# A chunked gated recurrence inside a projection kernel: its attention levels regrouped into tiles of 32 keys, with a compact block for the masked copies

## The chip, the cores and the metric

One NeuronCore of a Trainium2 chip. The metric is the device time of one execution in microseconds (us). Engines: TensorE (PE; its weight loads are PEld), VectorE (DVE), ScalarE (ACT), GpSimd (POOL), and SyncE (SP), which issues DMAs.

## The reference

One layer of a hybrid trunk over 2048 positions of 1024 channels, in float32: RMSNorm, one input projection, a pooling branch and a gated recurrence (HGRN2), each projected back and gated, an output projection, then a convolutional GLU feed-forward and a final norm. The change touches the recurrence alone. Its core, for each of 4 heads of 128 channels:

```python
f = lb + (1 - lb) * sigmoid(zf); k = 1 - f; q = silu(zq); v = zi
# S_t = diag(f_t) S_{t-1} + k_t v_t^T ;  o_t = S_t^T q_t , in chunks:
b = cumsum(log f)                               # inside a chunk
attn[t, s] = sum_k q[t,k] * exp(b[t,k] - b[s,k]) * k[s,k]   for s <= t
o = attn @ v + (q * exp(b)) @ state
state = exp(b_last) * state + (k * exp(b_last - b))^T @ v
```

## The kernel before, in words

The large projections are float32 products made of three fp32r matmuls each (high and low parts), in Strassen-like units of seven products; all of them are issued by one helper (L150), and the weights are split on the way by a ScalarE cast (L246) and a VectorE subtraction (L247). The sequence is worked in two halves of 1024 positions; each half has a mixer and a feed-forward part, and each mixer holds two blocks of 512 positions (four pieces of 128).

The recurrence runs as small tasks beside the mixer's projections: one `hgrn_task` for each of 4 heads and 4 blocks, 16 in all, up to three at a time, the two blocks of one head usually in step. Python generators stand for the tasks: after every six matmuls of the helper the loop advances each task that is due, and `yield n` means "not before n such ticks". So a task's instructions land between projection matmuls in the program, and `in_turn` holds a task's first matmul of a level behind the projection matmul that was issued last. A scheduler that simulates times sets the final order on each engine; each engine then works its queue in order.

Inside a task, q, k (`ks`) and the decays d (the f above) lie as channels by 512 positions. The 128x128 causal block `att` (keys by queries, four pieces side by side) is built by levels: at level h, queries of the upper half of each block of 2h positions meet keys of its lower half, with q and k scaled by the decays between. After each level q, k and d are updated, so that the next level needs only a product. Before the change the levels are:

- Levels 1 and 2 (L1106): four matmuls each, 128 keys by 128 moving columns; half of the columns also deliver the diagonal. Two masked copies from PSUM into `att`, each of 256 elements on 128 partitions (L1113, L1126).
- Levels 4+8 (`two_levels`, hh = 4): operands from ScalarE (L1042), GpSimd (L1043) and VectorE (L1044, L1047, L1049), in halves of two pieces. 16 matmuls (L1060) of 32 keys by 48 moving columns, in four groups of 32 PSUM partitions. 12 masked copies of 32 partitions by 64 elements (L1074). Then VectorE updates q, k and d.
- Levels 16+32 (hh = 16): the same with 8 matmuls of 64 keys by 96 columns and 6 masked copies of 64 partitions by 128 elements.
- Level 64: four matmuls of 64 keys by 64 columns (L1119) and one ScalarE copy (L1124), without a mask, as the whole rectangle is wanted.

Then k is transposed (L1140), the state products (L1149) and the outputs (L1165, L1167) follow, and the result goes to DRAM for the next projection. The masks are made at the start on GpSimd (`setup_task`, L638 to L656), between DMAs that accumulate weights (L167).

Of the kernel before, what the change touches and what calls it, by code (L numbers as in the profile page):

```python
# [13 lines left out]
U8 = mybir.dt.uint8  # L14
AF = mybir.ActivationFunctionType
ALU = mybir.AluOpType
AX = mybir.AxisListType

P = 128
# [11 lines left out]
NT = TB // P  # L31
# [41 lines left out]
AHEAD = 3  # L73
ADD_LAG = 3
# [9 lines left out]
def tile_trunk(  # L84
# [541 lines left out]
    def setup_task():  # L626
# [6 lines left out]
        keys = [(h, h, 0, h) for h in (1, 2, 4, 16)]  # L633
        keys += [(8 * h + t, 2 * h, t * h, h) for h in (4, 16) for t in range(2)]
        for key, x, off, w in keys:
            nb = 64 // x
            mf = mask_of()
            behind(pool.memset(mf, 1.0), last_root[0] if len(masks) < 6 else added[3])  # L638
            v = mf.rearrange("p (b h) -> p b h", h=x)
            pool.affine_select(out=v, in_=v, pattern=[[-2 * x, nb], [0, x]],  # L640
                               compare_op=ALU.is_ge, fill=0.0, base=-off, channel_multiplier=1)
            pool.affine_select(out=v, in_=v, pattern=[[2 * x, nb], [0, x]],
                               compare_op=ALU.is_ge, fill=0.0, base=off + w - 1,
                               channel_multiplier=-1)
            m8 = const.tile([P, 64], U8, tag=f"m{key}", name=f"m{key}")
            yield 2
            pool.tensor_copy(m8, mf)
            masks[key] = m8.rearrange("p (b h) -> p b h", h=x)
        for t in range(2):
            mf = mask_of()  # L650
            behind(pool.memset(mf, 0.0), added[3])
            pool.affine_select(out=mf, in_=mf, compare_op=ALU.not_equal, fill=1.0, base=-t,
                               pattern=[[-2, 64]], channel_multiplier=1)
            m8 = const.tile([P, 64], U8, tag=f"md{t}", name=f"md{t}")
            yield 2
            pool.tensor_copy(m8, mf)  # L656
            masks[-1 - t] = m8.unsqueeze(1)
# [339 lines left out]
    def hgrn_task(b, h, d, q, vd, zd, od):  # L997
        def head_of(src, key):
# [11 lines left out]
        qe, qo = (q.rearrange("p (c b t) -> p c b t", c=NT, t=2)[:, :, :, t] for t in range(2))  # L1010
        de, do = (d.rearrange("p (c b t) -> p c b t", c=NT, t=2)[:, :, :, t] for t in range(2))
        ae, ao = (att.rearrange("p (c b t) -> p c b t", c=NT, t=2)[:, :, :, t] for t in range(2))
        q1, q2 = (slot(f"q{i}{b}_{h}").rearrange("p (c s x) -> p c s x", c=NT, s=2)
                  for i in (1, 2))
        act.copy(q1[:, :, 1], qe)
        act.copy(q2[:, :, 1], qo)
        dve.tensor_tensor(q1[:, :, 0], qo, do, ALU.mult)
        dve.tensor_tensor(qe, qe, de, ALU.mult)
        dve.tensor_tensor(qo, q1[:, :, 0], de, ALU.mult)
        yield 3  # L1020
        def mask(key, n):
            m = masks[key]
            return m.unsqueeze(1).to_broadcast([P, n, m.shape[1], m.shape[2]])

        def two_levels(hh):
            nb = P // (4 * hh)
            d5 = d.rearrange("p (c b t h) -> p c b t h", c=NT, t=4, h=hh)
            q5 = q.rearrange("p (c b t h) -> p c b t h", c=NT, t=4, h=hh)
            qv = q.rearrange("p (c b t h) -> p c b t h", c=NT, t=2, h=hh)
            av = att.rearrange("p (c b t h) -> p c b t h", c=NT, t=2, h=hh)  # L1030
            av2 = att.rearrange("p (c b t h) -> p c b t h", c=NT, t=2, h=2 * hh)
            q2 = q.rearrange("p (c b t h) -> p c b t h", c=NT, t=2, h=2 * hh)
            mvs = {}
            for i in range(0, NT, 2):
                cc = slice(i, i + 2)
                mv = (slot(f"qm{b}_{h}_{hh}_{i}")[:, :384]
                      .rearrange("p (c s x) -> p c s x", c=2, s=3))
                near = mv[:, :, 0].rearrange("p c (b h) -> p c b h", h=hh)
                half = mv[:, :, 1].rearrange("p c (b t h) -> p c b t h", t=2, h=hh)
                far = [mv[:, :, 1 + t].rearrange("p c (b h) -> p c b h", h=2 * hh)  # L1040
                       for t in range(2)]
                act.copy(near, qv[:, cc, :, 1, :])  # L1042
                pool.tensor_copy(half[:, :, :, 0, :], q5[:, cc, :, 2, :])  # L1043
                dve.tensor_tensor(half[:, :, :, 1, :], q5[:, cc, :, 3, :],  # L1044
                                  d5[:, cc, :, 2, 0:1].to_broadcast([P, 2, nb, hh]), ALU.mult)
                full = [P, 2, nb, 2 * hh]
                dve.tensor_tensor(far[1], far[0], d5[:, cc, :, 1, 0:1].to_broadcast(full),  # L1047
                                  ALU.mult)
                dve.tensor_tensor(q2[:, cc, :, 1, :], far[1],  # L1049
                                  d5[:, cc, :, 0, 0:1].to_broadcast(full), ALU.mult)  # L1050
                mvs[i] = mv
            yield AHEAD
            w = 32 if hh == 4 else 64
            n = P // w
            x = w // 2
            pa_ = bank(f"pl{b}_{h}_{hh}", NT * 3 * x)
            ps = pa_.rearrange("p (c s x) -> p c s x", c=NT, s=3)
            for c in range(NT):
                for g in range(n):
                    ins = pe.matmul(ps[g * w : g * w + w, c],  # L1060
                                    ks[:, c * P + g * w : c * P + g * w + w],
                                    mvs[c // 2 * 2][:, c % 2, :, g * x : g * x + x],
                                    start=True, stop=True)
                    if not (c or g):
                        in_turn(ins)
            yield 1
            for g in range(n):
                r = slice(g * w, g * w + w)

                def put(to, key, s, k):  # L1070
                    m = masks[key][r, g * (x // k) : (g + 1) * (x // k)]
                    m = m.unsqueeze(1).to_broadcast([w, NT, x // k, k])
                    to = to[r, :, g * (x // k) : (g + 1) * (x // k), 1, :]
                    dve.copy_predicated(to, m, ps[r, :, s].rearrange("p c (b h) -> p c b h", h=k))  # L1074

                put(av, hh, 0, hh)
                for t in range(2):
                    put(av2, 8 * hh + 1 - t, 1 + t, 2 * hh)
# [11 lines left out]

        for lv in (0, 1, 2, 4, 6):
            hh = 1 << lv
            if lv in (2, 4):
                yield from two_levels(hh)
                continue
            nb = P // (2 * hh)
            qv = q.rearrange("p (c b t h) -> p c b t h", c=NT, t=2, h=hh)
            av = att.rearrange("p (c b t h) -> p c b t h", c=NT, t=2, h=hh)
            if lv < 2:
                qd, ad = ((q1, ae), (q2, ao))[lv]  # L1100
                if lv == 1:
                    act.copy(q2[:, :, 0].rearrange("p c (b h) -> p c b h", h=2), qv[:, :, :, 1, :])
                    yield AHEAD
                pa_ = bank(f"pl{b}_{h}_{hh}")
                for c in range(NT):
                    ins = pe.matmul(pa_[:, c * P : (c + 1) * P], ks[:, c * P : (c + 1) * P],  # L1106
                                    qd[:, c].rearrange("p s x -> p (s x)"),
                                    start=True, stop=True)
                    if not c:
                        in_turn(ins)  # L1110
                yield 2
                pv4 = pa_.rearrange("p (c s x) -> p c s x", c=NT, s=2)
                dve.copy_predicated(ad, masks[-1 - lv].to_broadcast([P, NT, 64]), pv4[:, :, 1])  # L1113
                pv4 = pv4[:, :, 0].rearrange("p c (b h) -> p c b h", h=hh)
            else:
                yield AHEAD
                pa_ = bank(f"pl{b}_{h}_{hh}", 256)
                for c in range(NT):
                    ins = pe.matmul(pa_[:hh, c * hh : (c + 1) * hh], ks[:, c * P : c * P + hh],  # L1119
                                    qv[:, c, 0, 1, :], start=True, stop=True)  # L1120
                    if not c:
                        in_turn(ins)
                yield 2
                act.copy(av[:hh, :, 0, 1, :], pa_[:hh].rearrange("p (c h) -> p c h", c=NT))  # L1124
            if lv < 2:
                dve.copy_predicated(av[:, :, :, 1, :], mask(hh, NT), pv4)  # L1126
            q3 = q.rearrange("p (b t h) -> p b t h", t=2, h=hh)
            k3 = ks.rearrange("p (b t h) -> p b t h", t=2, h=hh)
# [888 lines left out]
```

## Time and profile before

| | us |
|---|---|
| median of 3 runs | 2504.39 (2503.92 to 2507.8) |
| the profiled execution | 2505.12 |
| its span, first to last instruction | 2503.4 |
| busy: PE, DVE, ACT, POOL | 2481.7, 2007.5, 1201.4, 814.5 |
| mean granted TensorE clock | 0.998 |

A line of the profile names the source line (L1060 is line 1060 of the kernel), the engine, the operation and the tiles (out<-in), then the shape and a count. For a matmul, `128*32 128x48` is 128 rows by 32 columns of weights and 128 rows by 48 moving columns; one float32 matmul leaves two records. Matmul durations overlap with those of their neighbours.

### The profile page before, as it was taken

Reading aid. Unit: us, or ns where it says so; the run is one execution under the profiler, and the core shown is the slowest. Engines: PE = TensorE matmul, PEld = TensorE weight load, DVE = VectorE, ACT = ScalarE, POOL = GpSimd, SP = SyncE. Lnnn points to the kernel's source line nnn. Section 1 sums busy time; section 2 is a strip of 40 time slices with the busy share of each in tenths; the row PEclk is TensorE's granted clock in tenths of the full one; section 3 lists DMA queues with packets and bytes.
Section 4 is the critical chain, followed back from the end, with each engine's and each line's share of the span. In section 5 each row is a group of like instructions: output and inputs, shape, how many; then the busy total and the mean of one; then the engine's idle time right before and its main releaser. Section 6 shows DMA issues by size and latency. Waiting matters only on the chain.

```text
span 2503.4 us, 36730 instructions
## 1 busy us (share of the span) xinstructions
PE 2481.7 (99%) x11940; PEld 2015.6 (81%) x11940; DVE 2007.5 (80%) x3606; ACT 1201.4 (48%) x2264; POOL 814.5 (33%) x1139
## 2 busy tenths in 40 slices
PE   9999999999999999999999999999999999999998
PEld 7877887887888888888888888888888888888887
DVE  7788778988898777885586888689979887778755
ACT  6524443434555544554455344443365555445534
POOL 4343353502354434461230212223033433325410
PEclk9999999999999999999999999999999999999999
DMA  8877888587898879997444343447443444447852
GB/s 274 272 196 235 245 226 244 190 251 250 197 262 231 233 226 238 266 362 246 135 147 155 111 135 110 144 148 258 138 146 123 154 149 138 148 136 245 322 165 100
DMA packets 257696, 497.75 MB, mean 199 GB/s; under 512 B 26912, under 2 KB 47520, under 8 KB 257184
## 3 DMA queue, kind: packets, MB, share of 16 engines
q1 hardware_dynamic: 189872, 317.53, 38.7%
q0 software_dynamic: 42656, 112.74, 17.6%
q10 hardware_dynamic: 24976, 65.13, 7.5%
q8 instruction: 94, 1.54, 0.2%
q14 instruction: 98, 0.80, 0.1%
HBM read 383.63 MB, written 189.27 MB: 229 GB/s over the span
## 4 chain that ended last, share of the span: by engine, by line
PE 91%; DVE 6%; issue 1%; POOL 1%; DMA 1%; ACT 0%; SPq 0%; ACTq 0%; DVEq 0%; POOLq 0%
PE dn_P L150 16%; PE up_Z L150 15%; PE up_X L150 10%; PE up_V L150 10%; PE wo_P L150 5%; PE pb L150 4%; PE gr_X L150 3%; PE gr_V L150 3%; PE io_Z L150 3%; PE io_V L150 2%; PE fr_X L150 2%; PE gr_Z L150 2%; PE fr_V L150 2%; PE gr_W L150 2%; DVE at L1074 1%; PE gr_Y L150 1%
## 5 line engine op out<-in xcount | busy, mean ns | idle before, releaser
L246 ACT CAST ops<-raw 128x512 fp32r<-128x512 f32 x792 | 488.0, 621 | 803.2 <-PE dn_P L150 177.8
L247 DVE TENSOR_TENSOR ops<-raw,ops 128x512 fp32r<-128x512 f32 x792 | 587.9, 746 | 196.6 <-ACT ops L246 182.3
L1751 DVE SCALAR_TENSOR_TENSOR e<-h,cols,e 128x512 f32<-128x512 f32 x176 | 143.1, 817 | 31.4 <-ACT e L1749 26.6
L1749 ACT ACTIVATE e<-h,cols 128x512 f32<-128x512 f32 x176 | 142.2, 814 | 25.3 <-DVE h L1199 18.1
L993 POOL DMA_DIRECT2D g_P<-dg_P x154 | 84.0, 547 | 160.7 <-PE dn_P L150 115.1
L1754 DVE SCALAR_TENSOR_TENSOR e<-h,cols,e 128x512 f32<-128x512 f32 x176 | 133.9, 770 | 2.5
L1320 POOL TENSOR_TENSOR gf_P<-e,e 128x512 f32<-128x512 f32 x44 | 61.2, 1393 | 150.4 <-DVE e L1760 93.2
L468 POOL TENSOR_TENSOR raw<-raw,raw 128x512 f32<-128x512 f32 x36 | 49.4, 1371 | 168.9 <-DVE ops L247 104.3
L1320 POOL TENSOR_TENSOR gf_P<-gf_P,e 128x512 f32<-128x512 f32 x44 | 59.3, 1347 | 72.0 <-DVE e L1760 71.6
L1744 POOL COPY h<-h 128x2 f32<-128x2 f32 x88 | 40.4, 471 | 118.1 <-DVE h L1198 111.1
L1746 POOL COPY hist<-h 128x2 f32<-128x2 f32 x88 | 35.3, 402 | 118.0 <-DVE h L1199 116.2
L1758 ACT ACTIVATE e<-e 128x512 f32<-128x512 f32 x88 | 55.6, 632 | 37.7 <-DVE e L1754 37.6
L1074 DVE COPY_PREDICATED at<-m,pl 32x64 f32<-32x64 uint8 (+1 forms) x288 | 68.6, 248 | 6.3
L1199 DVE TENSOR_TENSOR h<-up_u,up_V 128x512 f32<-128x512 f32 x88 | 60.1, 683 | 10.2 <-PE up_V L150 9.7
L1493 ACT ACTIVATE gt<-gt,cols 128x512 f32<-128x512 f32 x48 | 34.8, 725 | 69.6 <-DVE gt L1199 69.1
L1043 POOL COPY qm<-q 128x64 f32<-128x64 f32 x64 | 33.4, 549 | 98.5 <-DVE q L1049 26.7
L1295 DVE TENSOR_TENSOR x<-x,wo_P 128x512 f32<-128x512 f32 x88 | 55.8, 679 | 5.6 <-PE wo_P L150 5.2
L1295 DVE TENSOR_TENSOR ac<-ac,dn_P 128x512 f32<-128x512 f32 x72 | 47.1, 682 | 15.7 <-PE dn_P L150 15.3
L1460 POOL TENSOR_TENSOR q<-q,qs 128x512 f32<-128x512 f32 x16 | 21.9, 1367 | 113.2 <-ACT qs L1459 110.8
L1239 ACT COPY up_e<-up_X 128x512 f32<-128x512 f32 x44 | 25.8, 587 | 60.1 <-PE up_X L150 57.2
L1744 POOL COPY h<-hist 128x2 f32<-128x2 f32 x88 | 45.0, 518 | 28.6 <-DVE m_T42l L682 28.5
L1774 POOL DMA_DIRECT2D dg_P<-gf_P x88 | 50.8, 578 | 8.1 <-POOL gf_P L1320 7.4
(1334 smaller groups left out, 8016.9 us busy)
## 6 DMA issues: line engine op xcount, KB each, us to landing
g_P<-dg_P POOLq DMA_DIRECT2D x154, 256.0 KB, 5.9
raw<-in_w_up_t SPq DMA_DIRECT2D x132, 256.0 KB, 3.1
raw<-in_w_in_t SPq DMA_DIRECT2D x98, 256.0 KB, 3.5
dg_P<-gf_P POOLq DMA_DIRECT2D x88, 256.0 KB, 3.8
dg_P<-e SPq DMA_DIRECT2D x66, 256.0 KB, 3.6
raw<-in_w_dn SPq DMA_DIRECT2D x66, 256.0 KB, 3.6
x<-in_x SPq DMA_DIRECT2D x64, 256.0 KB, 5.1
gd<-gt ACTq DMA_DIRECT2D x64, 256.0 KB, 2.5
```

Source lines behind the costliest of these rows:

```text
L150: count[1] = pe.matmul(*args, **kw)
L246: self.mark = act.copy(hi, v)
L247: low = self.low = dve.tensor_tensor(lo, v, f32(hi), ALU.subtract)
L993: eng.dma_start(t, d)
L1074: dve.copy_predicated(to, m, ps[r, :, s].rearrange("p c (b h) -> p c b h", h=k))
L1199: return dve.tensor_tensor(dst, t, ps, ALU.add if how == "add" else ALU.subtract)
L1295: dve.tensor_tensor(t, t, ps[j], ALU.add if sg > 0 else ALU.subtract)
L1320: pin(eng.tensor_tensor(t, x0, x1, op))
L1744: pool.tensor_copy(h[:, 0:2], hist[:, mt] if hf == 0 else hs[s, 0][:, TB : TB + 2])
L1749: in_turn(act.activation(t, h[:, 2:], AF.Identity, bias=col(o_cb + mt), scale=col(o_cw + 4 * MF + mt)))
L1751: in_turn(second(dve.scalar_tensor_tensor(t, h[:, 1 : 1 + TB], col(o_cw + 2 * MF + mt), t, ALU.mult, ALU.add)))
L1754: dve.scalar_tensor_tensor(t, h[:, 0:TB], col(o_cw + mt), t, ALU.mult, ALU.add)
```

## The change

The levels become 1, 2+4, 8+16 and 32+64. Level 1 (with the diagonal) and the next two pairs are all computed in tiles of 32 keys: for each piece four matmuls, one for each group of 32 keys, with the near operand (32 moving columns) and four with the far one (16). That makes 32 matmuls a level where there were 4, 4, 16 and 8. All groups land in the same columns of PSUM, so that one masked copy on all 128 partitions serves the four groups: it writes into a compact block `ac`, the last 32 columns of each piece of `att`, where the diagonal block of the last group belongs. ScalarE then spreads the first three groups to their own columns. The operands of all four pieces are made at once; ScalarE copies what GpSimd copied. Levels 32+64 need no mask: 16 matmuls of 32 keys by 32 or 64 columns, and three ScalarE copies from PSUM to the right of the diagonal blocks. The masks shrink to 32 columns, are made for keys of 1, 2 and 8, and are cast group by group.

```diff
+GK = 32
+NG = 4
...
-        keys = [(h, h, 0, h) for h in (1, 2, 4, 16)]
-        keys += [(8 * h + t, 2 * h, t * h, h) for h in (4, 16) for t in range(2)]
+        keys = [(h, h, 0, h) for h in (1, 2, 8)]
+        keys += [(8 * h + t, 2 * h, t * h, h) for h in (2, 8) for t in range(2)]
...
-            pool.tensor_copy(m8, mf)
+            for g in range(NG):
+                r = slice(g * GK, g * GK + GK)
+                pool.tensor_copy(m8[r], mf[r, g * GK // 2 : (g + 1) * GK // 2])
...
+        qv, dv, av = (t.rearrange("p (c x) -> p c x", c=NT) for t in (q, d, att))
+        ac = av[:, :, P - GK : P]
...
+        def products(hh, near, far):
+            x = GK // 2
+            pa_ = bank(f"pl{b}_{h}_{hh}", NT * 3 * x)
+            ps = pa_.rearrange("p (c x) -> p c x", c=NT)
+            for c in range(NT):
+                for s in range(2):
+                    for g in range(NG):
+                        o = ps[g * GK : g * GK + GK, c]
+                        ins = pe.matmul(
+                            o[:, 2 * x :] if s else o[:, : 2 * x],
+                            ks[:, c * P + g * GK : c * P + g * GK + GK],
+                            far[:, c, g * x : g * x + x] if s else near(c, g),
+                            start=True, stop=True)
+                        if not (c or g or s):
+                            in_turn(ins)
+            return ps
+
+        def put(to, key, ps, k):
+            n = GK // 2 // k
+            m = masks[key].unsqueeze(1).to_broadcast([P, NT, n, k])
+            dve.copy_predicated(to, m, ps.rearrange("p c (b h) -> p c b h", h=k))
...
+        act.copy(qn.rearrange("p c s x -> p (c s x)"), q)
...
+        ps = products(1, lambda c, g: flat[:, c, g * GK : g * GK + GK], qf)
+        yield 2
+        dve.copy_predicated(ac, masks[0].rearrange("p x o -> p o x").to_broadcast([P, NT, GK]),
+                            ps[:, :, :GK])
+        put(halves(1), 1, ps[:, :, GK:], 1)
+        ke = ks.rearrange("p (c b t) -> p c b t", c=NT, t=2)[:, :, :, 0]
+        dve.tensor_tensor(ke, ke, do, ALU.mult)
+        dve.tensor_tensor(de, de, do, ALU.mult)
+
+        for hh in (2, 8, 32):
...
+            act.copy(qn[:, :, 0].rearrange("p c (b h) -> p c b h", h=hh),
+                     qv.rearrange("p c (b t h) -> p c b t h", t=2, h=hh)[:, :, :, 1, :])
+            act.copy(half[:, :, :, 0, :], q5[:, :, :, 2, :])
+            dve.tensor_tensor(half[:, :, :, 1, :], q5[:, :, :, 3, :],
+                              d5[:, :, :, 2, 0:1].to_broadcast([P, NT, nb, hh]), ALU.mult)
...
             yield AHEAD
...
+            if hh < GK:
+                x = GK // 2
+                ps = products(hh, lambda c, g: qn[:, c, :, g * x : g * x + x], qf)
+                yield 1
+                put(halves(hh), hh, ps[:, :, :x], hh)
                 for t in range(2):
-                    put(av2, 8 * hh + 1 - t, 1 + t, 2 * hh)
+                    put(halves(2 * hh), 8 * hh + 1 - t, ps[:, :, (1 + t) * x : (2 + t) * x], 2 * hh)
+            else:
+                for g in range(NG - 1):
+                    r = slice(g * GK, g * GK + GK)
+                    act.copy(av[r, :, r], ac[r])
+                pa_ = bank(f"pl{b}_{h}_{hh}", NT * 96)
+                ps = pa_.rearrange("p (c x) -> p c x", c=NT)
+                for c in range(NT):
+                    for g, to, w in ((0, slice(0, 32), qn[:, c, 0, :32]), (1, slice(0, 64), qn[:, c, 1]),
+                                     (2, slice(0, 32), qn[:, c, 0, 32:]), (0, slice(32, 96), qf[:, c])):
+                        ins = pe.matmul(ps[g * GK : g * GK + GK, c, to],
+                                        ks[:, c * P + g * GK : c * P + g * GK + GK], w,
+                                        start=True, stop=True)
...
+                yield 2
+                for g in range(NG - 1):
+                    r = slice(g * GK, g * GK + GK)
+                    to = av[r, :, (32, 64, 96)[g] :]
+                    act.copy(to, ps[r, :, : to.shape[2]])
```

The update of q, k and d at the end of a pair of levels is as before, now three times a task instead of twice; the separate loop over levels 1, 2 and 64 goes, and with it its waits in ticks: a task has 18 ticks of them ahead of the transposition of k where it had 23.

More of the change, by code (lines that the diff above doesn't have):

```diff
@@ L637, in setup_task @@
             mf = mask_of()
-            behind(pool.memset(mf, 1.0), last_root[0] if len(masks) < 6 else added[3])
+            behind(pool.memset(mf, 1.0), last_root[0] if len(masks) < 5 else added[3])
             v = mf.rearrange("p (b h) -> p b h", h=x)
@@ L644, in setup_task @@
                                channel_multiplier=-1)
-            m8 = const.tile([P, 64], U8, tag=f"m{key}", name=f"m{key}")
+            m8 = const.tile([P, GK // 2], U8, tag=f"m{key}", name=f"m{key}")
             yield 2
-            pool.tensor_copy(m8, mf)
+            for g in range(NG):
+                r = slice(g * GK, g * GK + GK)
+                pool.tensor_copy(m8[r], mf[r, g * GK // 2 : (g + 1) * GK // 2])
             masks[key] = m8.rearrange("p (b h) -> p b h", h=x)
[L649 to L657, printed above, removed]
+        m8 = const.tile([P, GK], U8, tag="md", name="md")
+        for g in range(NG):
+            r = slice(g * GK, g * GK + GK)
+            ins = pool.tensor_copy(m8[r], ident[r, r])
+            if not g:
+                behind(ins, added[3])
+        yield 2
+        masks[0] = m8.unsqueeze(2)
         pool.memset(hist, 0.0)
@@ L1008, in hgrn_task @@
         pool.memset(att, 0.0)
[L1010 to L1016, printed above, removed]
@@ L1017, in hgrn_task @@
-        dve.tensor_tensor(q1[:, :, 0], qo, do, ALU.mult)
-        dve.tensor_tensor(qe, qe, de, ALU.mult)
[L1019 to L1025, printed above, removed]
-            nb = P // (4 * hh)
[L1027 to L1051, printed above, removed]
-            yield AHEAD
[L1053 to L1076, printed above, removed]
-                for t in range(2):
-                    put(av2, 8 * hh + 1 - t, 1 + t, 2 * hh)
@@ new lines, in hgrn_task, with operands @@
+        qv, dv, av = (t.rearrange("p (c x) -> p c x", c=NT) for t in (q, d, att))
+        ac = av[:, :, P - GK : P]
+        def operands(hh):
+            near = slot(f"qn{b}_{h}_{hh}").rearrange("p (c s x) -> p c s x", c=NT, s=2)
+            far = slot(f"qf{b}_{h}_{hh}")[:, : NT * 64].rearrange("p (c x) -> p c x", c=NT)
+            return near, far
+        def products(hh, near, far):
[4 more added lines that the diff above has]
+                for s in range(2):
+                    for g in range(NG):
+                        o = ps[g * GK : g * GK + GK, c]
[7 more added lines that the diff above has]
+            return ps
@@ new lines, in put, with halves @@
+        def put(to, key, ps, k):
+            n = GK // 2 // k
+            m = masks[key].unsqueeze(1).to_broadcast([P, NT, n, k])
+            dve.copy_predicated(to, m, ps.rearrange("p c (b h) -> p c b h", h=k))
+        def halves(hh):
+            return ac.rearrange("p c (b t h) -> p c b t h", t=2, h=hh)[:, :, :, 1, :]
+        qe, qo = (qv.rearrange("p c (b t) -> p c b t", t=2)[:, :, :, t] for t in range(2))
+        de, do = (dv.rearrange("p c (b t) -> p c b t", t=2)[:, :, :, t] for t in range(2))
@@ new lines, in hgrn_task @@
+        qn, qf = operands(1)
+        act.copy(qn.rearrange("p c s x -> p (c s x)"), q)
+        dve.tensor_tensor(qf, qo, do, ALU.mult)
+        dve.tensor_tensor(qe, qe, de, ALU.mult)
+        dve.tensor_tensor(qo, qf, de, ALU.mult)
+        yield AHEAD
+        flat = qn.rearrange("p c s x -> p c (s x)")
+        ps = products(1, lambda c, g: flat[:, c, g * GK : g * GK + GK], qf)
+        yield 2
+        dve.copy_predicated(ac, masks[0].rearrange("p x o -> p o x").to_broadcast([P, NT, GK]),
+                            ps[:, :, :GK])
@@ L1089, in two_levels @@
             dve.tensor_tensor(dd[:, :, 0, 0:1], dd[:, :, 0, 0:1], dd[:, :, 1, 0:1], ALU.mult)
[L1091 to L1128, printed above, removed]
-            d3 = d.rearrange("p (b t h) -> p b t h", t=2, h=hh)
-            full = [P, NT * nb, hh]
-            if lv:
-                dve.tensor_tensor(q3[:, :, 1, :], q3[:, :, 1, :],
-                                  d3[:, :, 0, 0:1].to_broadcast(full), ALU.mult)
-            dve.tensor_tensor(k3[:, :, 0, :], k3[:, :, 0, :],
-                              d3[:, :, 1, 0:1].to_broadcast(full), ALU.mult)
-            dve.tensor_tensor(d3[:, :, 0, 0:1], d3[:, :, 0, 0:1], d3[:, :, 1, 0:1], ALU.mult)
```

14 lines of the change are left out of this document (added).

## The prediction

> **What bounds the kernel now.** I read the page first, then the two mixer stretches, then TensorE's order of instructions around the recurrence, then the waits.
>
> ```profile
> span 2503.4 us, 36730 instructions
> ...
> PE 2481.7 (99%) x11940; PEld 2015.6 (81%) x11940; DVE 2007.5 (80%) x3606; ACT 1201.4 (48%) x2264; POOL 814.5 (33%) x1139
> ...
> PE 91%; DVE 6%; issue 1%; POOL 1%; DMA 1%; ACT 0%; SPq 0%; ACTq 0%; DVEq 0%; POOLq 0%
> ```
>
> TensorE is busy throughout and carries 91% of the chain that ended last, so the end moves by what the change takes from TensorE's queue or adds to it: the recurrence's own matmuls, and TensorE's waits for it. VectorE at 80% matters where TensorE waits for it. The recurrence lies in two stretches of 340 us, one for each mixer; this is the first.
>
> ```profile
> 120.00:460.00 340.00, 332.59 (x1968) 269.43 (x1967) 280.77 (x705) 145.79 (x332) 139.96 (x152) 0.99 0.78 225
> ```
>
> Columns: stretch, length, then busy us of PE, PE's weight loads, DVE, ACT, POOL, then clock and DMA. DVE is 83% busy here, ACT 43%, PE idle 7.4 us.
>
> Matmul durations overlap, so I price a recurrence block by what it pushes back: the start of the projection matmul behind it, less the start of the one ahead of it, less the usual step of 0.23 us (119.97 to 120.20). A record below is half of a matmul: the four 128x128 matmuls of one level appear as eight.
>
> ```profile
> 119.97 0.40 PE L150 MATMUL gr_X<-x_f3h,ops 128*128 128x512 f32 x1
> 120.20 0.40 PE L150 MATMUL gr_Z<-x_T20h,ops 128*128 128x512 f32 x1
> ...
> 122.76 0.39 PE L150 MATMUL gr_Z<-x_T23h,ops 128*128 128x512 f32 x1
> 122.99 1.95 PE L1106 MATMUL pl<-q,k 128*128 128x128 f32 x16
> 124.69 0.48 PE L150 MATMUL gr_V<-x_T10h,ops 128*128 128x512 f32 x1
> 125.01 0.39 PE L150 MATMUL gr_V<-x_T10l,ops 128*128 128x512 f32 x1
> ...
> 140.22 0.40 PE L150 MATMUL gr_V<-x_B223h,ops 128*128 128x512 f32 x1
> 140.55 0.90 PE L1060 MATMUL pl<-qm,k 128*32 128x48 f32 x64
> 141.38 0.50 PE L150 MATMUL ur_X<-x_f0h,ops 128*128 128x512 f32 x1
> ...
> 224.02 0.40 PE L150 MATMUL gr_X<-x_f0h,ops 128*128 128x512 f32 x1
> 224.35 0.55 PE L1060 MATMUL pl<-qm,k 128*32 128x48 f32 x32
> 224.83 0.50 PE L150 MATMUL gr_X<-x_f1h,ops 128*128 128x512 f32 x1
> ...
> 306.90 0.40 PE L150 MATMUL ur_Z<-x_T23h,ops 128*128 128x512 f32 x1
> 307.22 1.54 PE L1060 MATMUL pl<-qm,k 128*64 128x96 f32 x32
> 308.69 0.50 PE L150 MATMUL ur_V<-x_T10h,ops 128*128 128x512 f32 x1
> ...
> 237.99 0.40 PE L150 MATMUL gr_X<-x_f4l,ops 128*128 128x512 f32 x1
> 238.31 0.68 PE L1119 MATMUL pl<-q,k 128*64 128x64 f32 x8
> 238.92 0.50 PE L150 MATMUL gr_X<-x_f4h,ops 128*128 128x512 f32 x1
> ```
>
> Two tasks run in step, so a block often holds two. The matmul behind a block is itself 0.09 us late (124.69 to 125.01 is 0.32), which I add each time. Levels 1 and 2: 124.69-122.76-0.23+0.09 = 1.79 us for a pair of tasks at one level. Levels 4+8 (four 32-column strips of the array): 1.02 for a pair (64 records), 0.67 for one task (32). So 32 more records cost 0.35 us, 11 ns each, and a block has a fixed part of 0.32. Four strips share the 11 ns, so in its strip a record takes 44 ns for 48 columns, 0.9 ns a column. Levels 16+32: 1.65 a pair. Level 64: 0.79 a task, one strip of 64 columns; its eight records take 0.68 us with a last one of 0.22 (its row is below), about 60 ns each, again 0.9 a column.
>
> **The change, part by part.**
>
> ```profile
> L1106 PE MATMUL pl<-q,k x256: 270/275/275, 123.0 to 1627.3; 128*128 128x128 f32 x128
> L1060 PE MATMUL pl<-qm,k x768: 206/206/298, 140.5 to 1642.8; 128*32 128x48 f32 x128, 128*64 128x96 f32 x64
> L1119 PE MATMUL pl<-q,k x128: 222/222/315, 155.5 to 1650.9; 128*64 128x64 f32 x128
> ```
>
> TensorE now. 256 records at L1106 are 16 pair blocks: 16 x 1.79 = 28.6. Levels 4+8 in 16 tasks, half paired: 4 x 1.02 + 8 x 0.67 = 9.4. Levels 16+32: 8 x 1.65 = 13.2. Level 64: 128 records are 16 blocks of 0.79 = 12.6. Together 63.8 us without waits.
>
> TensorE after. Levels 1, 2+4 and 8+16 become 32 matmuls each (64 records): 16 with 32 moving columns, 16 with 16, on all four strips in the order that the 4+8 form has now. At 0.9 ns a column a 32-column record takes 30 ns in its strip. For a 16-column one no row exists: 15 ns if columns alone count, 44 if the form has a floor at its present price. I take 28, just under the 32-column one, because a weight load of 32 columns stands behind each record and need not shrink. Each strip does 8 + 8 records a level: 8 x 30 + 8 x 28 = 0.46 us, plus 0.32 fixed: 0.78 alone, 1.24 for a pair. With half paired, a level costs 4 x 1.24 + 8 x 0.78 = 11.2; three cost 33.6. The last level (32+64) sends 32- and 64-column operands to the first strip, so that strip decides: per piece two records of 30 and two of 60, 180 ns, four pieces 0.72, plus 0.32 = 1.04; 16 tasks 16.6. Together 50.2. TensorE's own gain: 63.8 - 50.2 = 13.6 us. With 15 ns the three levels fall by 3 x 16 x 0.10 = 5 to a gain of 19; with 11 ns for each of 64 records (0.70 a level) they rise by 3 x 16 x 0.24 = 11.5 to a gain of 2.
>
> Against the 11 ns row stands a rule of the Trainium skill, TensorE: Matmul & The Clock Gate, Back-to-back issue gap: matmuls of 1 to 64 columns all cost about 60 cycles, a floor of about 25 ns from start to start. As one floor for the whole array it would make a level 64 x 0.025 + 0.32 = 1.9 us, an estimate, and the result 2543 instead of 2488 (rival 3); this trace has 64 records of 48 columns in 0.90 us, so here such a floor can hold inside one strip only, where it hardly differs from my 28.
>
> VectorE. Per task, 18 masked copies at L1074 and two each of the 256-element kind go; eight come (one of 128 elements, seven of 64), all 128 partitions high.
>
> ```profile
> L1074 DVE COPY_PREDICATED at<-m,pl x288: 205/228/310, 141.9 to 1656.0; 32x64 f32<-32x64 uint8 x103, 64x128 f32<-64x128 uint8 x41
> L1113 DVE COPY_PREDICATED at<-md,pl x32: 716/734/795, 124.5 to 1628.2; 128x256 f32<-128x256 uint8 x32
> L1126 DVE COPY_PREDICATED at<-m,pl x32: 709/761/798, 125.0 to 1629.1; 128x256 f32<-128x256 uint8 x32
> ...
> 416.01 0.75 PE L1119 MATMUL pl<-q,k 128*64 128x64 f32 x8 [3.39 <-DVE at L1074]
> ...
> 417.28 0.63 PE L150 MATMUL gr_X<-x_f7h,ops 128*128 128x512 f32 x1
> ...
> 419.84 0.39 PE L150 MATMUL gr_Y<-x_T41h,ops 128*128 128x512 f32 x1
> ...
> 411.26 5.71 DVE L1074 COPY_PREDICATED at<-m,pl 32x64 f32<-32x64 uint8 x22
> ...
> PE pl L1119 <- DVE at L1074: 4.2, 3, 3.4
> ```
>
> Copies: 18 x 0.24 + 2 x 0.73 + 2 x 0.76 = 7.3 us a task before, about 8 x 0.25 = 2.0 after; 16 tasks give VectorE 85 us. The multiplies stay about level: fewer and wider ones ahead of the products, a third set of updates behind them. Off the chain this is worth nothing. On it, it is worth the waits: at 416 TensorE stood 3.39 us behind 22 such copies in a row, and then six steps to 419.84 took 2.56 instead of 1.38 at a lowered clock. Waits of 4.2 plus 1.2 make 5.4. I count two thirds, 3.6, because the last level still waits for updates in the same queue; what is late next there is ScalarE's spreading copy.
>
> ScalarE and GpSimd. GpSimd's 64 copies of quarters (33.4 us busy) move to ScalarE, doubled in length; ScalarE also gets three spreading copies and three result copies a task.
>
> ```profile
> L1102 ACT COPY q<-q x16: 400/420/452, 122.7 to 1618.1; 128x256 f32<-128x256 f32 x16
> L1042 ACT COPY qm<-q x64: 281/294/306, 135.7 to 1637.0; 128x128 f32<-128x128 f32 x64
> L1043 POOL COPY qm<-q 128x64 f32<-128x64 f32 x64 | 33.4, 549 | 98.5 <-DVE q L1049 26.7
> ACT at L1124 <- PE pl L1119: 27.4, 13, 7.4
> L246 ACT CAST ops<-raw 128x512 fp32r<-128x512 f32 x80 | 49.2, 620 | 59.9 <-PE gr_V L150 14.7 <-PE ur_V L150 11.6 <-PE gr_Z L150 8.3
> ...
> 38.32 0.23 POOL L647 CAST m<-hist 128x64 uint8<-128x64 f32 x1
> 40.76 2.06 POOL L167 DMA_DIRECT2D raw<-in_w_io  x2 [2.21 <-DMA raw<-in_w_io]
> ```
>
> After: 0.62 for the first operand (as the cast of that size), 3 x (0.42 + 0.29) for the others, 3 x 0.29 spreading, about 1.2 for the last: 4.8 us a task; before 2.8 (three of 0.42, four of 0.29, one of 0.37). That is 32 us more in all, on an engine 43% busy here: zero, while the weight casts (L246) keep their lead. They mostly wait for TensorE to free a buffer, so they have one. The new copies wait in ScalarE's queue for VectorE and TensorE with casts behind them; today's last copy already waits up to 7.4 us for TensorE without a TensorE wait for a cast in this stretch. Mask making on GpSimd gets four short casts a mask: five masks ahead of 38.32 instead of six, about 2 us longer at 0.23 a cast, against 2.21 us idle before the accumulating loads at 40.76: zero, but that cover is then used up. The loads on SP keep their order.
>
> Sum: the profiled execution took 2505.12 us (span 2503.4), 0.7 above the median 2504.39. 2505.1 - 13.6 - 3.6 = 2487.9; I say 2488.
>
> **The rivals.**
> 1. Narrow records keep their present price of 11 ns: a gain of 2, with 3.6 of waits 2499.5. For it: no row is narrower than 48 columns; against: 96, 64 and 48 columns all give about 0.9 ns a column.
> 2. New waits eat it: ScalarE held by the spreading copies until casts are late, say four events like that at 416 (3.4 + 1.2 us): 2488 + 18 = 2506. For it: ScalarE waits at L1124 13 times; against: none of those reached TensorE.
> 3. Slower: the records of the new form do not overlap between strips, at TensorE. 3 x 16 x 64 = 3072 records go through the new levels; fixed parts and last level take 12 x 3 x 0.32 + 16.6 = 28.1, so the gain is gone at (63.8 - 28.1) / 3072 = 11.6 ns a record, barely above today's 11. At 22 ns, two strips at a time, it costs 32 us, less 3.6 of waits: 2533. By the 25 ns floor of that page it would be 2543, an estimate. Against it: four strips share their time now in the same order.
> 4. More than forecast: columns alone count (19), and all waits on VectorE go (5.4, and the state products' waits): 2479.
>
> **How the numbers follow.** Forecast (2482 to 2495) 0.57, rival 1 0.14, rival 2 0.10, rival 3 0.05, rival 4 0.14. A measurement here tells 0.2% (5 us) from no change: under 2499.4 is faster, over 2509.4 slower. Faster: forecast, rival 4 and half of rival 1, 0.78; same: the other half and half of rival 2, 0.12; slower: rival 3 and the other half, 0.10. The range 2475 to 2502 takes in rivals 1 and 4.
>
> **What would show it.** Blocks of 64 records for one task between projection matmuls that push back 0.7 to 0.8 us, and 16 last-level blocks near 1.0; masked copies near 0.25 us, 128 in all; no TensorE wait of over 1 us at the last level; ScalarE about 32 us busier, with TensorE waits for casts unchanged. Wrong if such a block takes over 1.0 us, or if TensorE is seen waiting for casts or for a spreading copy.

## The result, and the profile after

The changed kernel takes 2492.14 us (median of 4 runs, 2490.61 to 2492.51) where the kernel before took 2504.15 beside it: a ratio of 0.9948, interval 0.993 to 0.9965. That is 12.0 us faster; 16 were forecast. The profiled execution took 2491.93, its span 2490.1.

The page after, its lines on the span, the engines, the instruction queue of TensorE and the chain that ended last:

```profile
span 2490.1 us, 41224 instructions
...
PE 2464.5 (99%) x14372; PEld 2004.7 (81%) x14372; DVE 1924.1 (77%) x3318; ACT 1233.2 (50%) x2344; POOL 780.5 (31%) x1090
...
q8 instruction: 113, 1.85, 0.3%
...
PE 80%; DVE 3%; DMA 2%; issue 1%; ACT 0%; POOL 0%; SPq 0%; ACTq 0%; DVEq 0%; POOLq 0%
```

VectorE is 83.4 us lighter (85 forecast), ScalarE 31.8 heavier (32 forecast). New is the load on the queue q8: 113 packets where the page before has 94, 16 KB each (1.85 MB by 113), one for 256 instructions (14372 matmul records with their weight loads are 28744 instructions, or 112 packets).

Both mixers, in the columns of the prediction's row:

```profile
120.00:460.00 340.00, 328.75 (x3194) 267.17 (x3193) 240.41 (x563) 162.65 (x374) 127.98 (x120) 0.98 0.80 227
1350.00:1690.00 340.00, 339.64 (x3287) 279.64 (x3287) 236.14 (x576) 170.70 (x383) 52.67 (x65) 1.00 0.45 142
```

TensorE's idle time in the first mixer rose from 7.4 to 11.2 us at a clock of 0.98; in the second, with the same recurrence work and half the DMA load (0.45 against 0.80), it is 0.4 us. So the loss is looked for in the first one. TensorE's waits (line, waited for: total, times, longest):

```profile
PE pl L1029 <- issue: 4.7, 3, 2.9
PE gr_X L152 <- issue: 3.1, 1, 3.1
PE pl L1029 <- DVE qf L1078: 2.4, 2, 1.8
...
PE pl L1029 <- ACT qn L1049: 0.8, 1, 0.8
```

The waits at the last level for masked copies (4.2 us in before) are gone. In their place stand 7.8 us of "issue": TensorE waits for nothing that the profile shows, in four stops of 2.9, 0.5, 1.4 and 3.1 us. Before had no such row. An undisturbed block of two tasks at one of the three new levels (L1029), in the timeline of the second mixer:

```profile
1386.30 0.40 PE L152 MATMUL gr_V<-x_B221h,ops 128*128 128x512 f32 x1
1386.63 0.27 PE L1029 MATMUL pl<-qn,k 128*32 128x32 f32 x8
1386.71 0.23 PE L1029 MATMUL pl<-qf,k 128*32 128x16 f32 x8
1386.78 0.25 PE L1029 MATMUL pl<-qn,k 128*32 128x32 f32 x8
1386.84 0.23 PE L1029 MATMUL pl<-qf,k 128*32 128x16 f32 x8
...
1387.91 0.50 PE L152 MATMUL gr_V<-x_B221l,ops 128*128 128x512 f32 x1
1388.25 0.40 PE L152 MATMUL gr_V<-x_B221h,ops 128*128 128x512 f32 x1
```

By the prediction's reckoning it pushes back 1387.91-1386.30-0.23+0.11 = 1.49 us for 128 records; a last-level block of two tasks (64 records at L1098) comes to 1.71 in the same way. All 24 blocks of the three levels and all 8 of the last are such pairs; before, half were single.

Now the first mixer: a disturbed block, and a stop among projection matmuls:

```profile
138.26 0.27 PE L1029 MATMUL pl<-qn,k 128*32 128x32 f32 x8
...
142.44 0.30 PE L1029 MATMUL pl<-qf,k 128*32 128x16 f32 x6 [2.87 <-issue]
...
143.26 0.63 PE L152 MATMUL gr_V<-x_B222l,ops 128*128 128x512 f32 x1
143.69 0.63 PE L152 MATMUL gr_V<-x_B222h,ops 128*128 128x512 f32 x1
...
398.96 0.80 PE L152 MATMUL gr_X<-x_f1l,ops 128*128 128x512 f32 x1 [3.11 <-issue]
```

Ahead of 142.44 TensorE stood still inside a block, six records from its end, and nothing in the records held it. Behind this stop it works at a lower clock: steps of 0.43 us (143.26 to 143.69) instead of 0.23, with a granted clock of 0.50 from 142.5 to 145.5 us. The stop of 2.87 us so costs about 4.5, that of 3.11 about 6; behind those of 1.4 and 0.5 us the clock stayed at 1.00. The DMA view of two stretches, 138.2 to 140.0 us (first line) and 140.0 to 141.1 (the others); columns: queue, packets, MB, share of the engines:

```profile
q0 software_dynamic: 146, 0.30, 99.3%
...
q0 software_dynamic: 63, 0.13, 63.0%
...
q8 instruction: 1, 0.02, 5.5%
```

No instruction packet begins while GpSimd's accumulating transfers (q0) fill the engines; then one runs from 140.09 to 141.06, and TensorE goes on 1.4 us later. The same order stands at the other stops: a packet from 215.14 to 216.10 and work again at 217.45, one from 293.69 to 294.62 and work again at 296.09, one from 396.50 to 397.44 and work again at 398.96. This gave the theory for the experiments. A: TensorE runs out of instructions; a paired block of 128 records is 256 instructions, one packet, used up in 1.4 us, where projection matmuls take 128 x 0.23 = 29 us for one. B: the missing gain lies in the operand waits, at ScalarE and VectorE, and the "issue" is their shadow.

### The profile page after: what moved, and what is told of

Read it like the earlier page. It is cut to its first block, busy times and chain, and to the rows that moved or that the text cites. A ratio compares the mean times of both kernels' runs of the same rounds, so it can differ in the third digit from the quotient of the medians.

```text
span 2490.1 us, 41224 instructions
## 1 busy us (share of the span) xinstructions
PE 2464.5 (99%) x14372; PEld 2004.7 (81%) x14372; DVE 1924.1 (77%) x3318; ACT 1233.2 (50%) x2344; POOL 780.5 (31%) x1090
## 3 DMA queue, kind: packets, MB, share of 16 engines
q8 instruction: 113, 1.85, 0.3%
## 4 chain that ended last, share of the span: by engine, by line
PE 80%; DVE 3%; DMA 2%; issue 1%; ACT 0%; POOL 0%; SPq 0%; ACTq 0%; DVEq 0%; POOLq 0%
PE dn_P L152 17%; PE up_Z L152 15%; PE up_V L152 10%; PE up_X L152 10%; PE wo_P L152 5%; PE pb L152 3%; PE gr_X L152 2%; PE gr_V L152 2%; PE io_Z L152 1%; PE gr_Z L152 1%; PE gr_Y L152 1%; PE gr_W L152 1%; PE io_V L152 1%; PE fr_X L152 1%; PE fr_V L152 1%; DVE ops L249 1%
## 5 line engine op out<-in xcount | busy, mean ns | idle before, releaser
L1475 ACT ACTIVATE gt<-gt,cols 128x512 f32<-128x512 f32 x48 | 34.8, 725 | 42.8 <-DVE gt L1181 41.5
L718 POOL TENSOR_SCALAR ro<-so 128x4 f32<-128x4 f32 x16 | 5.0, 311 | 156.3 <-ACT sq L1154 156.1
L1616 POOL TENSOR_TENSOR ya<-ya,gl 128x512 f32<-128x512 f32 x24 | 36.7, 1552 | 26.2 <-DVE ya L1613 14.8
```

## The experiments

All ratios are to the kernel before, run beside each; the kernel after the change stands at 0.9948. The kernel before took from 2504.2 to 2506.1 us in these comparisons, so between two runs the ratios say more than the microseconds.

**Instruction supply: more records.** Both records of each far matmul are issued twice, the second time over the first: 1536 more records, nothing else.

```diff
-                for s in range(2):
+                for s in (0, 1, 1):
```

> Changed kernel with every far matmul of 16 columns of levels 1, 2+4 and 8+16 issued twice, same operands and same result: 1536 records more, 12 pages of instructions more. Array time: 32 more records a task and level at 8 ns, 48 x 0.26 = 12 us. Theory A: the issue waits in the first mixer at least double (8 us idle to 16 or more) and the time is 2515 to 2525; packets on queue 8 near 125. Theory B: the array time alone, 2504.

Measured: 2536.55 us (2535.05 to 2538.26), ratio 1.013 (1.0116 to 1.0144), 44 us above the kernel after. TensorE's waits:

```profile
PE pl L1029 <- issue: 28.0, 8, 5.3
PE gr_X L152 <- issue: 3.3, 3, 1.5
```

the instruction queue on its page:

```profile
q8 instruction: 125, 2.05, 0.3%
```

and the projection matmuls around an undisturbed block (192 records between the first two), from its timeline:

```profile
1406.83 0.40 PE L152 MATMUL gr_X<-x_f5h,ops 128*128 128x512 f32 x1
1408.97 0.50 PE L152 MATMUL gr_X<-x_f5l,ops 128*128 128x512 f32 x1
1409.30 0.39 PE L152 MATMUL gr_X<-x_f5h,ops 128*128 128x512 f32 x1
```

The block without a stop pushes back 2.01 us instead of 1.49: 64 records of 16 columns for 0.52 us, 8.1 ns each, 33 ns in their strip. Over 24 blocks that is 12.5 us; the rest of the 44 are 32.2 us of "issue" (0.9 more in a third row) where there were 7.8, now in the second mixer too, and the lowered clock behind them. Waits for operands at the products (3.6 us) stay near what they were (3.2). Theory A is borne out, with an effect larger than its 2515 to 2525; B's 2504 is excluded.

Taken together, the traces say it more sharply. Those of the kernel after and of the experiments have 25 issue waits in all. Behind every one of them TensorE goes on 1.22 to 1.54 us after an instruction packet has ended. And if the records of TensorE are counted in order (matmuls, weight loads and semaphore instructions), every one stands 193 or 194 records behind a multiple of 256, that is at the same edge between two packets. So these waits are missing instructions, in the bursts and in the plain matmuls behind them.

**Instruction supply: bursts apart.** A task waits five ticks instead of three between the making of its operands and their product. That gives the operands more lead, and parts the two tasks of a pair.

```diff
-AHEAD = 3
+AHEAD = 5
```

> Changed kernel with AHEAD 5 instead of 3: two ticks (about 2.8 us) more between a level's operands and its matmuls. Theory A: the three issue waits (7.8 us idle) stay, the waits of TensorE for VectorE and ScalarE at the level products (about 4 us idle with slow clock behind them) go: 2487, 2484 to 2490. Theory B: all waits at the level products go, about 15 us: 2477.

Measured: 2487.2 us (2486.34 to 2488.59), ratio 0.9933 (0.9921 to 0.9946). TensorE's waits:

```profile
PE pl L1029 <- issue: 2.9, 1, 2.9
...
PE po L1149 <- DVE ss L1139: 1.8, 1, 1.8
```

and the projection matmuls around a block of one task (64 records between the first two), from its timeline:

```profile
206.81 0.39 PE L152 MATMUL gr_X<-x_f7h,ops 128*128 128x512 f32 x1
207.82 0.50 PE L152 MATMUL gr_X<-x_f7l,ops 128*128 128x512 f32 x1
208.16 0.39 PE L152 MATMUL gr_X<-x_f7h,ops 128*128 128x512 f32 x1
```

The time is the 2487 of theory A, but it did not come about in A's way: A had the issue waits stay. Of their 7.8 us 2.9 are left, inside a block that is still paired (it starts at 393.13 us); no wait for an operand is left at the products. Half of the work is now in single blocks, which push back 0.89 us each. In a pair the second 64 records add 1.49-0.89 = 0.60 us, 9.4 ns each, so a block has a fixed part of 0.29, which every parted pair pays once more; and still the kernel is faster: by 5 us, though the interval overlaps that of the kernel after (0.993 to 0.9965).

**Is the longer lead a gain without the change?** The same edit in the kernel before.

> The kernel before (2504.2) with AHEAD 5, nothing else. If the gain of AHEAD 5 in the changed kernel is peculiar to it, this does nothing but move the last level's wait (4.2 us idle and 1.2 of slow clock): 2499 to 2504. Rival (a longer lead alone would have given the kernel before the same as the change did): 2492.

Measured: 2502.1 us (2501.09 to 2504.87), ratio 0.9986 (0.9977 to 0.9995). The wait for masked copies goes there too, others come:

```profile
PE po L1167 <- DVE ss L1157: 3.7, 4, 1.7
PE pv L1149 <- ACT kt L1142: 3.6, 2, 2.3
```

So the lead is worth about 4 us there (1 to 6 by the interval), and the rival's 2492 is excluded: with the longer lead in both kernels the change is still worth 0.9986 to 0.9933, some 13 us. What the lead took away after the change, the issue waits, the kernel before does not have.

**Instruction supply: less traffic beside it.** The sums of weights that GpSimd's accumulating transfers make are planned at half their rate.

```diff
-SUM_LAG = 7
+SUM_LAG = 14
```

> Changed kernel with SUM_LAG 14 instead of 7: the DMAs of 1 MB that make weight sums run at half the rate, so that the DMA engines are less busy in the first mixer (0.80 now) and busier later. Theory A: instruction pages come sooner in the first mixer (delays of up to 7.5 us fall to some 3), the issue waits shrink from 7.8 us idle to under 3: 2484 to 2489, unless sums come late for the projections behind the mixer. Theory B: the issue waits stay, 2492.

Measured: 2537.07 us (2530.89 to 2537.32), ratio 1.0124 (1.0108 to 1.014). The first mixer:

```profile
120.00:460.00 340.00, 331.67 (x3226) 269.73 (x3225) 247.36 (x572) 165.05 (x379) 123.51 (x117) 0.99 0.64 196
```

and four of TensorE's waits in the whole span:

```profile
PE dn_P L152 <- ACT dn_P_2h L684: 7.8, 1, 7.8
PE up_Z L152 <- DVE up_u L1230: 6.4, 1, 6.4
...
PE pl L1029 <- issue: 3.1, 2, 2.4
...
PE gr_X L152 <- issue: 1.4, 1, 1.4
```

With the DMA share at 0.64 instead of 0.80 the issue waits fall from 7.8 to 4.5 us; A asked for under 3. Between 460 and 1350 us TensorE is now idle for 36 us instead of 1, which costs far more and fits sums that come too late for the later projections (dn_P and others). The packets hardly came sooner. Counted from a fixed place in TensorE's order (208 records behind each edge between two packets, a place that every packet follows by 0.6 us or more), those of the first mixer began 3.9 us later at the median and 7.8 at most in the kernel after, and 3.2 and 7.3 here; in the second mixer of the kernel after it was 1.3 and 2.8. What makes a packet late is therefore only partly answered: at 140 us the engines were full, but ahead of the packet at 396.50 no transfer of any queue began between 392.9 and 395.3 us. The share alone does not decide either: a kernel further below, with the longer lead, has 0.82 and no issue wait.

**Fewer matmuls.** Near and far operand stand side by side in one tile, and one matmul of 48 columns takes the place of two: 16 matmuls a level instead of 32.

```diff
-                for s in range(2):
-                    for g in range(NG):
...
-                            far[:, c, g * x : g * x + x] if s else near(c, g),
+                for g in range(NG):
...
+                                    mv[c // 2][:, c % 2, :, g * x : g * x + x],
```

> Changed kernel (2492.1 us), but near and far operands lie side by side (two tiles of two pieces each) and go through the array in one matmul of 48 columns per group: 64 records fewer for each pair of tasks and level, 1536 in all. Theory A (TensorE runs out of instructions: a paired block of 128 records empties a 16 KB page of them in 1.4 us, and in the first mixer the page's DMA starts up to 7.5 us late): a paired block falls from 1.48 to the 1.02 us of the old 4+8 form (24 x 0.46 = 11 us), instruction packets on queue 8 fall from 113 to about 101, and the waits marked issue (7.8 us idle, about 4 more at the lowered clock) go: 2470, 2465 to 2477. Theory B (these are waits for operands that the profile does not name): the 11 us alone, the issue waits stay: 2481. Rival 3 of the prediction in mild form (a record costs the same whatever its width): a block falls to half its moving part, 0.9 us.

Measured: 2485.97 us (2480.88 to 2486.93), ratio 0.9923 (0.991 to 0.9935). The instruction queue on its page:

```profile
q8 instruction: 101, 1.65, 0.3%
```

and TensorE's longest waits:

```profile
PE pl L1103 <- DVE qm L1082: 4.5, 3, 3.2
PE pl L1026 <- DVE qm L1082: 3.7, 1, 3.7
```

With 12 packets fewer the profiled execution (2480.88 us) has no issue wait at all, and an undisturbed pair block falls to 1.02 us, both as A said. But the operands are now made in two pieces, by more instructions, and waits for VectorE and ScalarE took the place: 12.0 us at the products where there were 3.2. A's 2470 is missed by 16 us, 11 in the profiled execution, since it put these at nothing; what the median execution had beyond the profiled one, no trace shows.

**Both.** The merged matmuls with the longer lead.

> The kernel with near and far in one matmul (2486.0) with AHEAD 5. Theory A (few instructions, so no issue waits; what is left is TensorE waiting for VectorE and ScalarE operands, 11 us idle with slow clock behind some of them): these waits go as they did in the changed kernel with AHEAD 5, issue waits stay away: 2473, 2470 to 2477. Rival (merging gave only its array time, and the waits left are of a kind that a longer lead does not help): 2484 to 2487.

Measured: 2481.6 us (2479.91 to 2482.42), ratio 0.9899 (0.9885 to 0.9912). Waits at the products shrink to 1.2 + 0.8 + 0.5 us, but single waits of 2.3 for the state (po), 2.3 for ScalarE's result copy and 2.2 for a gate are left: 9 us above A's 2473 and outside its range, below the rival's.

**Masked copies.** The matmuls of the changed kernel, but the seven copies that go by half blocks issued for each group of 32 partitions: 29 copies a task instead of 8.

```diff
-            m = masks[key].unsqueeze(1).to_broadcast([P, NT, n, k])
-            dve.copy_predicated(to, m, ps.rearrange("p c (b h) -> p c b h", h=k))
+            for g in range(NG):
+                r = slice(g * GK, g * GK + GK)
+                m = masks[key][r].unsqueeze(1).to_broadcast([GK, NT, n, k])
+                dve.copy_predicated(to[r], m, ps[r].rearrange("p c (b h) -> p c b h", h=k))
```

> Changed kernel (2492.1) with the masked copies that go by half blocks issued once for each group of 32 partitions, as the kernel before did: 29 a task instead of 8, all else as changed. Theory (fewer copies relieve VectorE by 5 us a task, which is worth only the waits of TensorE for VectorE): VectorE about 75 us busier, TensorE's waits for VectorE at the products grow from 2.4 us to about 10: 2500, 2496 to 2506. Rival (the copies are hidden anyway): 2492.

Measured: 2571.15 us (2568.1 to 2573.15), ratio 1.0256 (1.0242 to 1.027); 71 us above the expectation. The engines on its page:

```profile
PE 2494.3 (97%) x14372; PEld 2023.5 (79%) x14372; DVE 2021.9 (79%) x3654; ACT 1235.6 (48%) x2344; POOL 777.4 (30%) x1090
```

and TensorE's longest waits:

```profile
PE pl L1100 <- DVE qf L1080: 18.1, 7, 3.4
PE pl L1029 <- DVE k L1118: 17.0, 9, 3.0
PE pl L1100 <- DVE k L1118: 8.3, 8, 1.3
```

VectorE has 336 more instructions and 97.8 us more work, 0.29 us for each. A copy of a quarter of the partitions is no cheaper than one of all: the median at its line is 0.226 us, against 0.221. VectorE's total is about that of before (2007.5). Yet TensorE now waits over 40 us for it: between two levels stand all copies of the one and all operands of the next. So here the copies were not hidden, and without the one copy for four groups that the compact block allows, the change would have been a loss.

**ScalarE or GpSimd.** One of the three operand copies (L1073) goes back to GpSimd.

```diff
-            act.copy(half[:, :, :, 0, :], q5[:, :, :, 2, :])
+            pool.tensor_copy(half[:, :, :, 0, :], q5[:, :, :, 2, :])
```

> Changed kernel with the copy of the half operand on GpSimd again instead of ScalarE (48 copies of 128x128). Theory (ScalarE has room): no change, 2490 to 2494. Rival 2 of the prediction (ScalarE's queue holds back casts or operands): TensorE's waits for ScalarE go and it is 2 to 4 us faster.

Measured: 2486.29 us (2481.88 to 2486.76), ratio 0.9915 (0.9901 to 0.9928): 6 us faster than the kernel after, where no change was expected. Its waits:

```profile
PE pl L1029 <- ACT qn L1049: 2.1, 2, 1.3
...
PE gr_X L152 <- issue: 1.7, 1, 1.7
...
PE pl L1029 <- issue: 1.0, 2, 0.6
```

Operand waits did not fall (2.4 + 0.8 us after; 2.1 + 1.0 + 0.6 here); issue waits fell from 7.8 to 2.7. To tell whether this is a gain of its own, the edit was joined with the longer lead, and with the merged matmuls and the longer lead.

> The kernel after the change with half of the near operand's copy on GpSimd and AHEAD 5. Theory A (both edits take away the same issue waits of TensorE, and each alone has left one to three): their gains do not add up, 2484 to 2487, at most 3 us below either. Rival B (ScalarE's operand copies are a cost of their own beside the instruction supply): the gains add up, 5 and 6 us, to about 2481.

> The merged matmuls with AHEAD 5, and half of the near operand's copy on GpSimd instead of ScalarE. Theory A (TensorE no longer runs out of instructions here, and what is left are single waits for ScalarE and VectorE operands): ScalarE 1.2 to 1.6 us a task lighter helps those waits by 1 to 3 us: 2479 (2476 to 2482). Rival B (the gain of GpSimd in the kernel after the change came only from moving the tasks, so that their matmul bursts fell elsewhere): 2481 to 2484, no change against the same kernel without GpSimd.

Measured: 2481.42 us (2479.08 to 2482.7), ratio 0.9909 (0.9893 to 0.9926), and 2475.36 us (2471.54 to 2475.71), ratio 0.988 (0.9865 to 0.9895). In all three pairs the copy on GpSimd is better, by 8, 6 and 5 us going by the ratios (0.9948 to 0.9915, 0.9933 to 0.9909, 0.9899 to 0.988), against A's expectation that the gains would not add; B's 2481 is met, and the second kernel lies below the ranges of both its theories. The intervals of the first pair lie apart, those of the other two overlap by 0.0005 and 0.001. But what goes is not a wait for ScalarE. The first of these two kernels in the first mixer:

```profile
120.00:460.00 340.00, 337.76 (x3250) 272.67 (x3249) 257.76 (x578) 162.53 (x362) 148.20 (x152) 1.00 0.82 236
```

Against the longer lead alone, the issue wait of 2.9 and the wait of 1.8 for the state are gone; TensorE is idle for 2.2 us in this stretch instead of 6.0 (the profiled execution took 2479.08, 2 us less than the median). The cost of ScalarE's copy is thus shown in its size, 5 to 8 us, and not in its way: a lighter ScalarE, or another order of the tasks that parts the bursts; that stays open. The kernel with all three edits, 29 us faster than the one before the change, is the best of all.

## Why the prediction was right, and the step that failed

The time lay in the range, 4 us from the forecast. That it lay so near is in part luck: several terms were off and largely cancelled. Adding up, over the whole trace, what every block between projection matmuls pushes back (us):

| | before | after | difference |
|---|---|---|---|
| levels, undisturbed blocks | 67.1 | 49.1 | -18.0 |
| waits and lowered clock at the levels | 4.8 | 11.0 | +6.2 |
| state and output matmuls | 46.9 | 42.8 | -4.1 |
| transpositions of k and the result | 16.0 | 14.4 | -1.6 |
| transpositions of the norms | | | -0.6 |
| other waits among projection matmuls | | | +4.7 |

The sum is -13.4, the spans differ by 13.3.

- **TensorE's own gain**, forecast 13.6, was 18.0. After: 24 pair blocks of 1.475 and 8 of 1.71 us (means) are 49.1, forecast 50.2. Inside this a record was too cheap: 33 ns in its strip for 16 columns (forecast 28), and 38 as a mean of both widths (pair less single, 0.60 us for 16 records a strip; forecast 29). At 1386.63 the groups of eight follow each other by 0.08, 0.07, 0.06, so the width hardly counts. A single block came to 0.89 us (forecast 0.78), a pair to 1.49 (1.24). Rival 1's 11 ns a record against the forecast's 7 is met half way, at 8.1 to 9.4. What made up for it is that all tasks now run in pairs, which was put at half; so the 18.0 is near rival 4's 19, but not in its way. The 60 ns that the prediction reads for a record of 64 columns are 66 by its own row ((0.68 - 0.22) / 7), 1.0 ns a column. The term for before, 63.8, was too small by 3.3; 2.7 of this lie at levels 16+32, where it priced single tasks as half a pair each; some blocks there were also split in two. For a single task:

```profile
1474.00 0.40 PE L150 MATMUL gr_Z<-x_T23h,ops 128*128 128x512 f32 x1
1474.33 0.88 PE L1060 MATMUL pl<-qm,k 128*64 128x96 f32 x16
1475.14 0.51 PE L150 MATMUL gr_V<-x_T10h,ops 128*128 128x512 f32 x1
1475.48 0.39 PE L150 MATMUL gr_V<-x_T10l,ops 128*128 128x512 f32 x1
```

  This block of before pushes back 1.02 us, not 0.83.
- **Waits**, forecast -3.6: this is the step that failed. The waits at the last level went, as said, but 7.8 us of missing instructions and 3.2 us of waits for operands at the products came, with a lowered clock behind them, and the sum is +6.2 and +4.7. No rival had this cause: the instruction supply stands nowhere in the prediction. Rival 2 had the form (new waits, some four stops of 3 us with slow steps behind), and put the blame on ScalarE's spreading copies. Those (L1092) held up weight loads for 2.1 us in all; no matmul's wait in the kernel after names them, and the one wait for a cast (io_Z) went from 0.5 to 0.9 us.
- **State and output matmuls and transpositions** were left out of the sum, and gave 5.7: their waits for VectorE's state (2.4 in before) went, and pairs share the fixed part.
- **VectorE and ScalarE**: right in size. The copies:

```profile
L1041 DVE COPY_PREDICATED at<-m,pl x112: 209/221/325, 125.6 to 1625.8; 128x64 f32<-128x64 uint8 x112
```

  Each takes 0.22 us, forecast 0.25. The forecast took the 85 us to be worth the waits alone, 3.6 us; but with 98 put back beside these products, 77 came back on the time (by the ratios), so in the new form the copies, in that number, stand on the chain. That ScalarE's added copies cost zero is not borne out: one of the three operand copies alone, moved to GpSimd, gave 5 to 8 us, in a way that stays open.
- **Rival 3**, records that do not overlap between strips, is excluded by 8 to 9 ns a record. The Trainium skill's floor of about 25 ns from start to start (TensorE: Matmul & The Clock Gate, Back-to-back issue gap) is compatible with the 33 ns inside a strip, and not with 8 ns across the array.

## What to carry to other kernels

Price a burst of small matmuls by its instructions too: as many as the projections use in 29 us were used in 1.4, and the stops came not only in the burst but in the plain matmuls behind it. A masked copy costs its instruction and its free size (0.22 us for 64 elements, 0.73 for 256), not its partitions (0.23 us on 32, 0.22 on 128), so a layout that lets all groups of partitions share one copy may be worth more than the matmuls it rearranges. When two tasks may or may not run in step, price both cases for the kernel before and after.

## What the runs showed of the hardware

Instruction supply was not expected to matter. In the kernel after, TensorE idled 0.4 us in the second mixer, and the first had 7.8 us of stops, at 113 packets in the whole run; with 125 packets there were 32.2 us over both mixers. The packet itself takes 0.93 to 0.97 us at the stops of the kernel after, and TensorE went on 1.4 to 1.5 us behind its end. After the two stops of about 3 us the granted clock was 0.50, and the 512-column matmuls followed each other by 0.43 us instead of 0.23, for 6 and for 11 matmuls. The Trainium skill says (Runtime: NRT & Kernel Launch, Instruction fetch mechanics) that an engine's instructions are fetched in blocks of 16 KiB while it works, and calls the crossing of a block "mostly hidden". The size agrees with the 16 KB of a q8 packet here. The hiding held in the second mixer of the kernel after, and not in the first.
